# Tying the 32-column operations of the state-space parameters to VectorE's order in the first MLP's first part

## The chip, the cores and the metric

One core of one Trainium2 chip runs the whole program. The metric is the device time of one execution in microseconds (us): the median of several runs.

## The reference, cut to what matters

A causal decoder trunk of two layers on a sequence of 512 tokens of width 1024, all in float32. Each layer is a mixer and a gated MLP, both with a residual add behind an RMS norm. Layer 0 mixes by a convolution and attention, layer 1 by a state-space model (S5) whose parameters are worked out from 32 groups of 64 complex states.

```python
def conv_ffn(xn, w_up, conv_w, conv_b, w_down):          # width 2816, conv over 3 tokens
    h = causal_dwconv(xn @ w_up, conv_w, conv_b)
    return (jax.nn.silu(h[..., :D_FF]) * h[..., D_FF:]) @ w_down

def s5_mixer(xn, w_in, log_dt, a_re, a_im, b_re, b_im, c_re, c_im, d_skip, w_glu, b_glu):
    u = (xn @ w_in).astype(f32).reshape(bsz, s, SSM_GROUPS, SSM_GROUP)
    dt = jnp.exp(log_dt.astype(f32))[:, None]
    mag = jnp.exp(ar * dt)
    lb_re, lb_im = mag * jnp.cos(ai * dt), mag * jnp.sin(ai * dt)
    den = ar * ar + ai * ai
    f_re = (nr * ar + ni * ai) / den        # nr, ni = lb_re - 1, lb_im; f_im likewise
    bb_re = f_re[..., None] * br - f_im[..., None] * bi
    ...                                     # scan over the sequence, output map, GLU

for i in range(2):
    x = x + mixer(rms_norm(x, mix_g), *mix_params)
    x = x + conv_ffn(rms_norm(x, ffn_g), *ffn_params)
return rms_norm(x, final_norm)
```

What `s5_mixer` does ahead of the scan (dt, mag, the cosines, lb, f, bb and powers of lb) depends on no token. It is needed only in layer 1.

## The kernel before, in words

**Layout and matmuls.** Activations lie transposed: channels on the 128 partitions, the 512 tokens along the free axis, so x is eight tiles of 128x512. Every product is made of three float32r matmuls (`mm3`: high weight by high input, high by low, low by high), called from `mm` (L109).

**Weights.** `chunk` hands out 128x1024 pieces of the weights in the fixed list `order`, two ahead of use (`LOOK`). For each, `load_w` issues one transfer on SyncE's queue into `raw` (L114, two buffers), ScalarE casts it into `whi` (L124, three buffers) and GpSimd makes the rest `wlo` in four subtractions of 128x256 (L126, three buffers).

**Order of the work.** Each engine runs its own list in order. The Tile framework's scheduler makes these lists from a simulated timeline; the code's order decides only what the data need and how ties fall. Instructions that are passed to `held` (`keep_in_program_order`) keep the code's order among themselves on their engine. In the kernel before no VectorE operation of the part in question is held.

**Ahead of the MLP.** The attention mixer ends with the out projection: TensorE makes eight `wo`, VectorE adds each to x (L657). Behind each add the norm goes on, in the class `Norm`: ScalarE makes the high part `xh` and the square `sq`, VectorE the low part `xl` (L273) and the running sum `ssq` (L291, L293, L298). Then `wide()` closes it: `total` splits the sum (`th` on ScalarE, `tl` on VectorE, L233) and adds it over the partitions on TensorE (`sum`, L235), VectorE makes `m` (L303) and three Newton steps (L226 to L228) of nine operations of 128x512, which give `rb`, the norm's factor. TensorE needs `xh` and `xl` for the MLP, but not `rb`.

**The MLP.** `ffn(l, ...)` runs in three `PARTS` of 8, 8 and 6 column pairs. For each pair there are two branches: an up projection into `ua` or `ug` (24 matmuls), then on VectorE `h` = PSUM times `rb` (L931), on ScalarE the first tap of the convolution back into PSUM (L932), and on VectorE two more taps (L934, 128x511 and 128x510). ScalarE makes `sl` = silu (L943), VectorE `g` = `sl` times `ug` (L946), ScalarE the cast `ghl` (L949), GpSimd its low half (L950). Behind the pairs of a part come eight down projections `dn`, which need the `ghl` of all pairs of the part, and VectorE adds them to x (L958). In layer 0's first two parts one step of the list `extra` is run behind each `dn`.

**The parameters.** `s5_tables` gives that list. It first calls `s5_small` (L762 to L815): some 180 VectorE operations of mostly 128x32 (exponentials, sines, reciprocals, complex powers and squarings) that depend on each other in chains, plus 128x64 and 128x128 ones. The eight batches of `s5_batch` follow (`bc` loaded on SyncE's queue, L863; `bb`, `bt`, `wn`, `w2` on VectorE; `en` and `e2` on GpSimd, L887 to L889; `park_O` written back, L896). In the kernel before `s5_small` is called at the head of `ffn`, outside any loop, and the scheduler places its operations where it likes.

Of the kernel before, what the change touches and what calls it, by code (L numbers as in the profile page):

```python
# [71 lines left out]
def trunk(ctx, tc, A, out):  # L72
# [617 lines left out]
        t = tpool.tile([128, n, NG], F32, tag=name, name=name)  # L690
        return t if n > 1 else t[:, 0]

    tt, ts, stt = v.tensor_tensor, v.tensor_scalar, v.scalar_tensor_tensor

    def exp_small(dst, a):
        MAGIC = 12582912.0
        xc, k, r, q = sm("xc"), sm("k"), sm("r"), sm("q")
        sc = sm("sc", I32)
        ts(xc, a, -87.0, 88.0, ALU.max, ALU.min)
        ts(k, xc, 1.4426950408889634, MAGIC, ALU.mult, ALU.add)  # L700
        ts(k, k, -MAGIC, None, ALU.add)
        stt(r, k, -0.693359375, xc, ALU.mult, ALU.add)
        stt(r, k, 2.12194440054690583e-4, r, ALU.mult, ALU.add)
        ts(q, r, 1.0 / 5040, None, ALU.mult)
        for c in (1.0 / 720, 1.0 / 120, 1.0 / 24, 1.0 / 6, 0.5, 1.0):
            stt(q, q, c, r, ALU.add, ALU.mult)
        ts(sc, k, 127.0, 8388608.0, ALU.add, ALU.mult)
        stt(dst, q, 1.0, sc.bitcast(F32), ALU.add, ALU.mult)

    def unit(c, sn):  # L710
        m, t = sm("m"), sm("t")
        tt(m, c, c, ALU.mult)
        tt(t, sn, sn, ALU.mult)
        tt(m, m, t, ALU.add)
        ts(m, m, -0.5, 1.5, ALU.mult, ALU.add)
        tt(c, c, m, ALU.mult)
        tt(sn, sn, m, ALU.mult)

    def sincos_small(c, sn, th):
        MAGIC = 12582912.0  # L720
        k, r, f, q, u = sm("k"), sm("r"), sm("f"), sm("q"), sm("u")
        ts(k, th, 0.15915494309189535, MAGIC, ALU.mult, ALU.add)
        ts(k, k, -MAGIC, None, ALU.add)
        stt(r, k, -6.28125, th, ALU.mult, ALU.add)
        stt(r, k, -0.0019340515136718750, r, ALU.mult, ALU.add)
        stt(r, k, -1.2556659146019e-06, r, ALU.mult, ALU.add)
        ts(r, r, 0.125, None, ALU.mult)
        tt(f, r, r, ALU.mult)
        ts(q, f, -1.0 / 5040, None, ALU.mult)
        stt(q, q, 1.0 / 120, f, ALU.add, ALU.mult)  # L730
        stt(q, q, -1.0 / 6, f, ALU.add, ALU.mult)
        stt(sn, q, 1.0, r, ALU.add, ALU.mult)
        ts(q, f, -1.0 / 40320, None, ALU.mult)
        stt(q, q, 1.0 / 720, f, ALU.add, ALU.mult)
        stt(q, q, -1.0 / 24, f, ALU.add, ALU.mult)
        stt(u, q, 0.5, f, ALU.add, ALU.mult)
        for _ in range(3):
            t = sm("t")
            stt(t, u, -1.0, sn, ALU.add, ALU.mult)
            stt(u, sn, 2.0, sn, ALU.mult, ALU.mult)  # L740
            ts(sn, t, -2.0, None, ALU.mult)
        ts(c, u, -1.0, 1.0, ALU.mult, ALU.add)
        unit(c, sn)

    def cmul(dr, di, ar, ai, br, bi, mk):
        t1, t2 = mk("cm1"), mk("cm2")
        tt(t1, ar, br, ALU.mult)
        tt(t2, ai, bi, ALU.mult)
        tt(dr, t1, t2, ALU.subtract)
        t3, t4 = mk("cm3"), mk("cm4")  # L750
        tt(t3, ar, bi, ALU.mult)
        tt(t4, ai, br, ALU.mult)
        tt(di, t3, t4, ALU.add)

    rho = keep("rho")
    fre, sfi = keep("fre"), keep("sfi")
# [4 lines left out]

    def s5_small():  # L762
        dt, e = sm("dt"), sm("e")
        exp_small(dt, ldt)
        tt(e, are, dt, ALU.mult)
        mag = keep("mag")
        exp_small(mag, e)
        th = sm("th")
        tt(th, aim, dt, ALU.mult)
        c, sn = keep("c"), keep("sn")  # L770
        sincos_small(c, sn, th)
        v.memset(pr[:, 0], 1.0)
        v.memset(pi[:, 0], 0.0)
        tt(pr[:, 1], mag, c, ALU.mult)
        tt(pi[:, 1], mag, sn, ALU.mult)
        nr, d1, d2 = sm("nr"), sm("d1"), sm("d2")
        ts(nr, pr[:, 1], -1.0, None, ALU.add)
        tt(d1, are, are, ALU.mult)
        tt(d2, aim, aim, ALU.mult)
        tt(d1, d1, d2, ALU.add)  # L780
# [3 lines left out]
        tt(a1, nr, are, ALU.mult)
        tt(a2, pi[:, 1], aim, ALU.mult)
        tt(a1, a1, a2, ALU.add)
        tt(fre, a1, rd, ALU.mult)
        a3, a4 = sm("a3"), sm("a4")
        tt(a3, pi[:, 1], are, ALU.mult)
        tt(a4, nr, aim, ALU.mult)  # L790
        tt(a3, a3, a4, ALU.subtract)
        stt(sfi, a3, s1, rd, ALU.mult, ALU.mult)
        for lo, n in ((1, 1), (2, 2), (4, 4)):
            def mk(name):
                return tpool.tile([128, 4, NG], F32, tag="cm", bufs=2, name=name)[:, :n]
            bc = [128, n, NG]
            cmul(pr[:, lo + 1:lo + 1 + n], pi[:, lo + 1:lo + 1 + n], pr[:, 1:1 + n], pi[:, 1:1 + n],
                 pr[:, lo:lo + 1].to_broadcast(bc), pi[:, lo:lo + 1].to_broadcast(bc), mk)
        ts(spr, pr, s1, None, ALU.mult)
        for j in range(CL):  # L800
            v.tensor_copy(prr[:, j], pr[:, CL - 1 - j])
            ts(spir[:, j], pi[:, CL - 1 - j], s1, None, ALU.mult)
        r2 = sm("r2")
        tt(r2, mag, mag, ALU.mult)
        tt(r2, r2, r2, ALU.mult)
        tt(rho, r2, r2, ALU.mult)
        g.memset(tab["D"][:, :, 0:1], 0.0)
        g.tensor_copy(tab["D"][:, :, 1:], rho.unsqueeze(2).to_broadcast([128, NG, NC - 1]))
        for n in range(8):
            dst = (sm("wa"), sm("wb")) if n < 2 else (wr[:, n - 2], wi[:, n - 2])  # L810
            t1, t2 = sm("t1"), sm("t2")
            tt(t1, c, c, ALU.mult)
            tt(t2, sn, sn, ALU.mult)
            tt(dst[0], t1, t2, ALU.subtract)
            stt(dst[1], c, 2.0, sn, ALU.mult, ALU.mult)  # L815
            unit(*dst)
# [490 lines left out]
```

## Time and the profile before

| what | us |
|---|---|
| median of three runs | 1070.20 |
| the three runs | 1069.37, 1070.20, 1074.71 |
| the profiled execution's own time | 1072.81 |
| its span | 1071.0 |
| TensorE busy | 1025.4 (96%) |
| VectorE busy | 660.5 (62%) |
| GpSimd busy | 680.1 (63%) |
| ScalarE busy | 447.5 (42%) |

The profiled execution's time is 1.8 us over its span, and 2.6 us over the median. Positions in the text are microseconds from the span's start. In a row of a timeline the first number is that position, the second how long the instruction took, and a bracket behind it is the engine's idle time just before and what ended it. In the profile's names PE is TensorE, PEld its weight loads, DVE VectorE, ACT ScalarE, POOL GpSimd, SP SyncE.

### The profile page before, as it was taken

To read this page: it belongs to the slowest core of one execution; us is meant where nothing else is said; L and a number is where in the kernel's file an instruction comes from. 1 tells how busy PE (TensorE), PEld (TensorE's weight loads), DVE (VectorE), ACT (ScalarE), POOL (GpSimd) and SP (SyncE) were. 2 spreads that over 40 slices of the span, in tenths; PEclk is the share of its full clock that TensorE was granted. 3 is DMA by queue.
4 is the path that set the end of the run, shared out by engine and by line. 5 is a ranking of instruction groups with operands and counts; after the bars stand their busy time and mean duration, and the time that the engine had idled before them with its cause. 6 is when DMAs were issued, how large, how long until landed. Compare 5 with 4: busy or idle time off the path is not lost.

```text
span 1071.0 us, 14173 instructions
## 1 busy us (share of the span) xinstructions
PE 1025.4 (96%) x4966; PEld 826.2 (77%) x4966; DVE 660.5 (62%) x1271; ACT 447.5 (42%) x665; POOL 680.1 (63%) x827
## 2 busy tenths in 40 slices
PE   7998999988999999999999778999999999999996
PEld 5876567766888888878888656888888888888895
DVE  7679974999647996368745485776521444214435
ACT  5476964413542335323444223535431444214431
POOL 4898955556776876678655552867755666556650
PEclk9999999999999999999999889999999999999998
DMA  5322202322333423233323641322223222232222
GB/s 194 112 96 79 60 21 68 112 74 79 105 111 105 134 86 129 83 120 122 114 84 116 229 135 50 119 98 99 99 85 112 99 99 99 79 111 94 96 75 79
DMA packets 54599, 108.66 MB, mean 101 GB/s; under 512 B 20609, under 2 KB 28417, under 8 KB 54529
## 3 DMA queue, kind: packets, MB, share of 16 engines
q1 hardware_dynamic: 54528, 107.77, 30.4%
q8 instruction: 39, 0.64, 0.2%
q14 instruction: 32, 0.25, 0.1%
HBM read 98.31 MB, written 8.39 MB: 100 GB/s over the span
## 4 chain that ended last, share of the span: by engine, by line
PE 75%; DVE 15%; ACT 3%; DMA 2%; issue 2%; POOL 2%; SPq 0%; DVEq 0%; POOLq 0%; ACTq 0%
PE ug L109 20%; PE dn L109 20%; PE ua L109 20%; PE gl L109 4%; PE win L109 3%; POOL wlo L126 2%; DVE acc L410 2%; PE pv L590 1%; PE wo L109 1%; PE sc L560 1%; PE w L109 1%; PE pt L574 1%; PE kb L907 1%; DMA raw<-w 1%; ACT whi L124 1%
## 5 line engine op out<-in xcount | busy, mean ns | idle before, releaser
L126 POOL TENSOR_TENSOR wlo<-raw,whi 128x256 fp32r<-128x256 f32 x639 | 485.4, 792 | 246.8 <-ACT whi L124 226.9
L124 ACT CAST whi<-raw 128x1024 fp32r<-128x1024 f32 (+1 forms) x162 | 167.0, 1035 | 291.4 <-PE dn L109 87.7
L109 PE MATMUL dn<-ghl,whi 128*128 128x512 f32 (+1 forms) x632 | 192.9, 387 | 0.0
L109 PE MATMUL ug<-xh,whi 128*128 128x512 f32 x352 | 138.0, 392 | 5.7 <-ACT whi L124 4.2
L109 PE MATMUL ua<-xl,whi 128*128 128x512 f32 x352 | 137.4, 390 | 1.9 <-DVE xl L273 1.9
L109 PE MATMUL ug<-xh,wlo 128*128 128x512 f32 x352 | 137.9, 392 | 0.2
L109 PE MATMUL ua<-xh,whi 128*128 128x512 f32 x352 | 137.6, 391 | 0.0
L109 PE MATMUL ug<-xl,whi 128*128 128x512 f32 x352 | 137.5, 391 | 0.0
L109 PE MATMUL ua<-xh,wlo 128*128 128x512 f32 x352 | 137.1, 390 | 0.0
L109 PEld LDWEIGHTS dn<-ghl,whi 128*128 128x128 f32 x632 | 117.3, 188 | 24.6 <-issue 0.8
L109 PE MATMUL dn<-ghl,wlo 128*128 128x512 f32 (+1 forms) x316 | 121.8, 386 | 0.0
L958 DVE TENSOR_TENSOR x<-x,dn 128x512 f32<-128x512 f32 x40 | 26.8, 683 | 108.8 <-PE dn L109 108.8
L934 DVE SCALAR_TENSOR_TENSOR ug<-h,vec,ug 128x511 f32<-128x511 f32 x88 | 66.2, 753 | 42.7 <-ACT ug L932 41.4
L934 DVE SCALAR_TENSOR_TENSOR ua<-h,vec,ua 128x511 f32<-128x511 f32 x88 | 66.3, 753 | 41.3 <-ACT ua L932 39.9
L109 PEld LDWEIGHTS ug<-xh,whi 128*128 128x128 f32 x352 | 66.4, 189 | 20.9 <-ACT whi L124 5.1
L950 POOL TENSOR_TENSOR ghl<-g,ghl 128x512 fp32r<-128x512 f32 x44 | 57.1, 1297 | 34.3 <-ACT ghl L949 34.3
L109 PEld LDWEIGHTS ua<-xl,whi 128*128 128x128 f32 x352 | 66.3, 188 | 16.0 <-DVE xl L273 2.4
L109 PEld LDWEIGHTS ug<-xh,wlo 128*128 128x128 f32 x352 | 66.2, 188 | 14.7 <-POOL wlo L126 1.1
L109 PEld LDWEIGHTS ua<-xh,whi 128*128 128x128 f32 x352 | 66.1, 188 | 14.2 <-issue 0.6
L109 PEld LDWEIGHTS ug<-xl,whi 128*128 128x128 f32 x352 | 66.3, 188 | 13.7
L109 PEld LDWEIGHTS ua<-xh,wlo 128*128 128x128 f32 x352 | 66.2, 188 | 13.8
L109 PEld LDWEIGHTS dn<-ghl,wlo 128*128 128x128 f32 x316 | 59.4, 188 | 11.7
(343 smaller groups left out, 1788.0 us busy)
## 6 DMA issues: line engine op xcount, KB each, us to landing
raw<-up SPq DMA_DIRECT2D x88, 512.0 KB, 3.2
raw<-down SPq DMA_DIRECT2D x32, 512.0 KB, 3.3
raw<-w SPq DMA_DIRECT2D x14, 512.0 KB, 3.7
raw<-down SPq DMA_DIRECT2D x16, 384.0 KB, 2.9
raw<-wg SPq DMA_DIRECT2D x8, 512.0 KB, 3.5
raw<-wo_a SPq DMA_DIRECT2D x4, 512.0 KB, 3.2
raw<-wo_c SPq DMA_DIRECT2D x4, 512.0 KB, 4.2
park_O<-wn SPq DMA_DIRECT2D x8, 256.0 KB, 2.6
```

The source lines that it names most:

```text
L109: r = pe.matmul(*a, **kw)
L124: s.copy(hi[:, :n], r)
L126: (eng or g).tensor_tensor(lo[:, a:a + 2], r[:, a:a + 2], hi[:, a:a + 2].bitcast(F32), ALU.subtract)
L410: held(v.scalar_tensor_tensor(acc[:, sh:], u[:, :T - sh], col("cw", i * CK + CK - 1 - sh), acc[:, sh:], ALU.mult, ALU.add))
L560: pe.matmul(ps[:, :L], q[:, sl], k[:, :L], start=True, stop=False)
L574: pe.transpose(pt[:, kt * 128:(kt + 1) * 128], p[:, kt * 128:(kt + 1) * 128], ident)
L590: pe.matmul(ps[a, kt * 128:], vv[:, kt, i * 128 + 64 * e:i * 128 + 64 * e + 64], pts[e][:, 4 * kt:3 * kt + 4].rearrange("p k c -> p (k c)" ...
L907: pe.matmul(kb[0:16, i * 128:(i + 1) * 128], bb[:, i], wn[:, i, 0:8].rearrange("p j c -> p (j c)"), start=True, stop=True)
L934: v.scalar_tensor_tensor(ps[:, sh:], t[:, :T - sh], col(fw, 3 * j + 2 - sh), ps[:, sh:], ALU.mult, ALU.add)
L950: g.tensor_tensor(lo, gt, h.bitcast(F32), ALU.subtract)
L958: v.tensor_tensor(x[m], x[m], ps, ALU.add)
```

## The change

The functions of the small operations (`exp_small`, `unit`, `sincos_small`, `cmul`, `s5_small`) become generators that stop behind each operation. `pin` wraps `tensor_tensor`, `tensor_scalar` and `scalar_tensor_tensor`, so that the operation is `held` while `pinned[0]` is set, which it is from the head of `s5_small` to its end. `ffn` no longer calls them at once: `drip(14)` takes 14 steps ahead of each branch in every part, which lasts for the 16 branches of the first part, since there are 185 steps; `drip(1000)` ahead of the down projections takes what is left. No instruction is added or removed on any engine. All VectorE operations of the new code that go through `pin` are shown as L698.

```diff
+DRIP = 14
...
-    tt, ts, stt = v.tensor_tensor, v.tensor_scalar, v.scalar_tensor_tensor
+    pinned = [False]
+
+    def pin(op):
+        def run(*a):
+            r = op(*a)
+            return held(r) if pinned[0] else r
+        return run
+
+    tt, ts, stt = pin(v.tensor_tensor), pin(v.tensor_scalar), pin(v.scalar_tensor_tensor)
...
-        tt(m, c, c, ALU.mult)
-        tt(t, sn, sn, ALU.mult)
+        yield tt(m, c, c, ALU.mult)
+        yield tt(t, sn, sn, ALU.mult)
...
     def s5_tables(bp):
-        s5_small()
+        pinned[0] = True
+        yield from s5_small()
+        pinned[0] = False
...
-        return todo
+        yield todo
...
     def ffn(l, nrm, nxt, extra=None):
         rb = nrm.wide()
         fw, fb = f"fw{l}", f"fb{l}"
-        extra = [] if extra is None else extra(fp)
+        steps, extra = extra and extra(fp), []
+
+        def drip(n):
+            for _ in range(n):
+                r = next(steps, 0) if steps else 0
+                if r == 0:
+                    return
+                if isinstance(r, list):
+                    extra.extend(r)
...
             for i in range(i0, i0 + n):
+                drip(DRIP)
                 pa = branch(2 * i, bank("ua"))
                 sl = tmp("sl")
                 s.activation(sl, pa, AF.Silu)
+                drip(DRIP)
                 pg = branch(2 * i + 1, bank("ug"))
...
+            drip(1000)
             for m in range(KD):
```

What that does to the engines' lists is seen at three places. On VectorE, at the end of the out projection, the small operations stood between the adds and the norm's operations (numbers behind `x_`, `d_` and `cm_` are tile numbers):

```order
L657 TENSOR_TENSOR x_84<-x_84,wo 128x512
L715 TENSOR_SCALAR m<-m 128x32
L716 TENSOR_TENSOR c<-c,m 128x32
L717 TENSOR_TENSOR sn<-sn,m 128x32
L774 TENSOR_TENSOR pr<-mag,c 128x32
L775 TENSOR_TENSOR pi<-mag,sn 128x32
L777 TENSOR_SCALAR nr<-pr 128x32
L273 SCALAR_TENSOR_TENSOR xl<-x_82,vec,xh 128x512
L778 TENSOR_TENSOR d_2152<-ssm_small 128x32
```

Now that stretch of the list holds the adds and the norm alone up to the first branch:

```order
L299 TENSOR_TENSOR ssq<-ssq,sq 128x512
L234 TENSOR_TENSOR tl<-ssq,th 128x512
L304 TENSOR_SCALAR m<-sum 128x512
L225 TENSOR_SCALAR rb<-m 128x512
L227 TENSOR_TENSOR q<-rb 128x512
L228 SCALAR_TENSOR_TENSOR q<-q,m 128x512
L229 SCALAR_TENSOR_TENSOR rb<-q,rb 128x512
...
L698 TENSOR_SCALAR xc<-ssm_small 128x32
L952 TENSOR_TENSOR h<-ua,rb 128x512
```

Of the small operations only the first (`xc`) and one `wn` stay ahead of the first `h`; 206 of the 208 that stood there have gone. They stand between the branches' operations, up to the 16th branch. On VectorE at the tenth branch, where before only `h`, two taps and `g` stood, the list reads:

```order
L952 TENSOR_TENSOR h<-ug,rb 128x512
L698 TENSOR_TENSOR pi<-cm_2388,cm_2389 128x32
L698 TENSOR_TENSOR m<-m,t 128x32
L698 TENSOR_TENSOR cm_2393<-pr 128x64
L698 TENSOR_TENSOR cm_2394<-pi 128x64
L698 TENSOR_SCALAR spir<-pi,vec 128x32
L698 TENSOR_SCALAR m<-m 128x32
L698 TENSOR_TENSOR pr<-cm_2393,cm_2394 128x64
...
L955 SCALAR_TENSOR_TENSOR ug<-h,vec,ug 128x511
```

About 14 small operations stand in each branch, more in branches 8 to 11. On SyncE's queue the second `bc` and the first `park_O` stood among the loads of the up projection's weights:

```order
L114 DMA raw<-up 128x1024 x5
L863 DMA bc<-ssm_bc 128x256
L114 DMA raw<-up 128x1024
L896 DMA park_O<-wn 128x4x128
L114 DMA raw<-up 128x1024 x10
L114 DMA raw<-down_0 128x1024 x7
```

Now they follow all of these loads of the first part:

```order
L115 DMA raw<-up 128x1024 x16
L876 DMA bc<-ssm_bc 128x256
L909 DMA park_O<-wn 128x4x128
L115 DMA raw<-down_0 128x1024 x7
```

GpSimd's copy of `tabD`, `en` and `e2` move from ahead of the first low half of `ghl` to between the fourth and the sixth. From the first `dn` on, all five lists are as before.

## Rows read from the trace of the kernel before

**Rows 1.** The page's first section: busy time of each engine, its share of the span, instructions.

```profile
PE 1025.4 (96%) x4966; PEld 826.2 (77%) x4966; DVE 660.5 (62%) x1271; ACT 447.5 (42%) x665; POOL 680.1 (63%) x827
```

**Rows 2.** Busy time of each engine from the first `ua` to the first `dn` of the first MLP, and of the second MLP (layer 1, without parameter operations).

```profile
core 0: us, PE busy (x) PEld busy (x) DVE busy (x) ACT busy (x) POOL busy (x), PEclk, DMA share, GB/s
203.66:303.47 99.81, 91.30 (x388) 73.14 (x387) 87.81 (x229) 39.20 (x53) 62.65 (x75) 0.98 0.26 88
696.39:783.89 87.50, 87.50 (x388) 72.46 (x387) 55.01 (x72) 41.38 (x55) 58.62 (x72) 1.00 0.29 98
```

**Rows 3.** TensorE's timeline in the first of these stretches: three matmuls that waited.

```profile
209.83 0.50 PE L109 MATMUL ua<-xl,whi 128*128 128x512 f32 x1 [1.93 <-DVE xl L273]
239.09 0.50 PE L109 MATMUL ug<-xh,whi 128*128 128x512 f32 x1 [2.76 <-ACT whi L124]
252.05 0.50 PE L109 MATMUL ug<-xh,whi 128*128 128x512 f32 x1 [1.43 <-ACT sl L943]
```

**Rows 4.** SyncE's queue and ScalarE's timeline: when the second `bc` was issued, and the weight cast that waited behind it.

```profile
234.12 0.33 SPq L863 DMA_DIRECT2D bc<-ssm_bc  x1
237.99 1.05 ACT L124 CAST whi<-raw 128x1024 fp32r<-128x1024 f32 x1 [18.35 <-DMA raw<-up]
```

**Rows 5.** VectorE's timeline: the first and the last instruction of the stretch in which it had no idle time, and the busy times of all engines between them.

```profile
180.65 0.18 DVE L699 TENSOR_SCALAR xc<-ssm_small 128x32 f32<-128x32 f32 x1 [1.54 <-DMA ssm_small<-ssm]
266.78 0.68 DVE L931 TENSOR_TENSOR h<-ua,rb 128x512 f32<-128x512 f32 x1
180.65:266.78 86.13, 77.62 (x328) 61.79 (x327) 84.89 (x258) 27.52 (x36) 46.78 (x56) 0.98 0.30 96
```

**Rows 6.** VectorE's timeline among the last Newton operations: two small operations and a wide one (L228), which show the step from one start to the next.

```profile
242.97 1.27 DVE L812 TENSOR_TENSOR t<-wr 128x32 f32<-128x32 f32 x1
...
247.39 0.68 DVE L228 SCALAR_TENSOR_TENSOR rb<-q,rb 128x512 f32<-128x512 f32 x1
247.99 0.18 DVE L712 TENSOR_TENSOR m<-wr 128x32 f32<-128x32 f32 x1
```

**Rows 7.** VectorE's costliest groups from 180 to 266 us: line, operation, tile, shape, count, busy us, mean ns of one, idle before.

```profile
L273 DVE SCALAR_TENSOR_TENSOR xl<-x,vec,xh 128x512 fp32r<-128x512 f32 x8 | 6.4, 801 | 0.0
L657 DVE TENSOR_TENSOR x<-x,wo 128x512 f32<-128x512 f32 x8 | 5.4, 677 | 0.0
L293 DVE TENSOR_TENSOR ssq<-ssq,sq 128x512 f32<-128x512 f32 x5 | 3.4, 683 | 0.0
L227 DVE SCALAR_TENSOR_TENSOR q<-q,m 128x512 f32<-128x512 f32 x3 | 2.6, 881 | 0.0
L226 DVE TENSOR_TENSOR q<-rb 128x512 f32<-128x512 f32 x3 | 2.6, 877 | 0.0
L934 DVE SCALAR_TENSOR_TENSOR ua<-h,vec,ua 128x511 f32<-128x511 f32 x2 | 1.5, 749 | 0.0
```

**Rows 8.** Three places of the second MLP (the twin): its last add to x, its first `h`, and what VectorE waited for in its first part (us in all, count, longest).

```profile
700.36 0.76 DVE L1143 TENSOR_TENSOR x<-x,gz 128x512 f32<-128x512 f32 x1
720.36 0.69 DVE L931 TENSOR_TENSOR h<-ua,rb 128x512 f32<-128x512 f32 x1
DVE ua L934 <- ACT ua L932: 7.7, 8, 1.7
DVE ug L934 <- ACT ug L932: 7.2, 7, 2.1
```

**Rows 9.** The same places in the first MLP, and the end of its first part: last add, first `h`, eighth `g`, its cast, its low half, and the first matmul that reads that.

```profile
211.71 0.67 DVE L657 TENSOR_TENSOR x<-x,wo 128x512 f32<-128x512 f32 x1
248.20 0.68 DVE L931 TENSOR_TENSOR h<-ua,rb 128x512 f32<-128x512 f32 x1
309.93 0.69 DVE L946 TENSOR_TENSOR g<-sl,ug 128x512 f32<-128x512 f32 x1
310.66 0.62 ACT L949 CAST ghl<-g 128x512 fp32r<-128x512 f32 x1 [2.33 <-DVE g L946]
311.35 1.28 POOL L950 TENSOR_TENSOR ghl<-g,ghl 128x512 fp32r<-128x512 f32 x1 [0.75 <-ACT ghl L949]
313.53 0.48 PE L109 MATMUL dn<-ghl,whi 128*128 128x512 f32 x1
```

**Rows 10.** Two short stretches, with GpSimd busy throughout and idle throughout, and one small operation of the first.

```profile
220.20:226.20 6.00, 5.35 (x24) 4.43 (x24) 6.00 (x10) 0.00 (x0) 6.00 (x8) 1.00 0.00 0
226.30:229.70 3.40, 3.40 (x17) 2.81 (x16) 3.40 (x28) 0.00 (x0) 0.00 (x0) 1.00 0.02 5
222.79 0.78 DVE L874 TENSOR_TENSOR bt<-bc,sfi 128x64 f32<-128x64 f32 x1
```

**Rows 11.** GpSimd's costliest group from 180.65 to 266.78 us, and two runs of weight subtractions from its timeline, the second in the twin.

```profile
L126 POOL TENSOR_TENSOR wlo<-raw,whi 128x256 fp32r<-128x256 f32 x51 | 38.7, 788 | 31.8 <-ACT whi L124 31.8
254.67 2.83 POOL L126 TENSOR_TENSOR wlo<-raw,whi 128x256 fp32r<-128x256 f32 x4 [1.12 <-ACT whi L124]
707.58 12.20 POOL L126 TENSOR_TENSOR wlo<-raw,whi 128x256 fp32r<-128x256 f32 x12 [5.17 <-ACT whi L124]
```

**Rows 12.** The granted clock (the column behind the engines) around the first wait of rows 3.

```profile
209.00:214.00 5.00, 4.17 (x11) 3.29 (x12) 5.00 (x17) 3.43 (x6) 2.73 (x3) 0.66 0.07 27
```

More of the change, by code (lines that the diff above doesn't have):

```diff
@@ L698, in exp_small @@
         sc = sm("sc", I32)
[L699 to L704, printed above, removed]
+        yield ts(xc, a, -87.0, 88.0, ALU.max, ALU.min)
+        yield ts(k, xc, 1.4426950408889634, MAGIC, ALU.mult, ALU.add)
+        yield ts(k, k, -MAGIC, None, ALU.add)
+        yield stt(r, k, -0.693359375, xc, ALU.mult, ALU.add)
+        yield stt(r, k, 2.12194440054690583e-4, r, ALU.mult, ALU.add)
+        yield ts(q, r, 1.0 / 5040, None, ALU.mult)
         for c in (1.0 / 720, 1.0 / 120, 1.0 / 24, 1.0 / 6, 0.5, 1.0):
-            stt(q, q, c, r, ALU.add, ALU.mult)
-        ts(sc, k, 127.0, 8388608.0, ALU.add, ALU.mult)
-        stt(dst, q, 1.0, sc.bitcast(F32), ALU.add, ALU.mult)
+            yield stt(q, q, c, r, ALU.add, ALU.mult)
+        yield ts(sc, k, 127.0, 8388608.0, ALU.add, ALU.mult)
+        yield stt(dst, q, 1.0, sc.bitcast(F32), ALU.add, ALU.mult)
     def unit(c, sn):
         m, t = sm("m"), sm("t")
-        tt(m, c, c, ALU.mult)
-        tt(t, sn, sn, ALU.mult)
[L714 to L717, printed above, removed]
+        yield tt(m, c, c, ALU.mult)
+        yield tt(t, sn, sn, ALU.mult)
+        yield tt(m, m, t, ALU.add)
+        yield ts(m, m, -0.5, 1.5, ALU.mult, ALU.add)
+        yield tt(c, c, m, ALU.mult)
+        yield tt(sn, sn, m, ALU.mult)
     def sincos_small(c, sn, th):
@@ L721, in sincos_small @@
         k, r, f, q, u = sm("k"), sm("r"), sm("f"), sm("q"), sm("u")
[L722 to L736, printed above, removed]
+        yield ts(k, th, 0.15915494309189535, MAGIC, ALU.mult, ALU.add)
+        yield ts(k, k, -MAGIC, None, ALU.add)
+        yield stt(r, k, -6.28125, th, ALU.mult, ALU.add)
+        yield stt(r, k, -0.0019340515136718750, r, ALU.mult, ALU.add)
@@ new lines, in sincos_small @@
+        yield stt(r, k, -1.2556659146019e-06, r, ALU.mult, ALU.add)
+        yield ts(r, r, 0.125, None, ALU.mult)
+        yield tt(f, r, r, ALU.mult)
+        yield ts(q, f, -1.0 / 5040, None, ALU.mult)
+        yield stt(q, q, 1.0 / 120, f, ALU.add, ALU.mult)
+        yield stt(q, q, -1.0 / 6, f, ALU.add, ALU.mult)
+        yield stt(sn, q, 1.0, r, ALU.add, ALU.mult)
+        yield ts(q, f, -1.0 / 40320, None, ALU.mult)
+        yield stt(q, q, 1.0 / 720, f, ALU.add, ALU.mult)
+        yield stt(q, q, -1.0 / 24, f, ALU.add, ALU.mult)
@@ L737, in sincos_small @@
+        yield stt(u, q, 0.5, f, ALU.add, ALU.mult)
         for _ in range(3):
             t = sm("t")
[L739 to L743, printed above, removed]
+            yield stt(t, u, -1.0, sn, ALU.add, ALU.mult)
+            yield stt(u, sn, 2.0, sn, ALU.mult, ALU.mult)
+            yield ts(sn, t, -2.0, None, ALU.mult)
+        yield ts(c, u, -1.0, 1.0, ALU.mult, ALU.add)
@@ L745, in cmul @@
+        yield from unit(c, sn)
     def cmul(dr, di, ar, ai, br, bi, mk):
         t1, t2 = mk("cm1"), mk("cm2")
-        tt(t1, ar, br, ALU.mult)
-        tt(t2, ai, bi, ALU.mult)
-        tt(dr, t1, t2, ALU.subtract)
+        yield tt(t1, ar, br, ALU.mult)
+        yield tt(t2, ai, bi, ALU.mult)
+        yield tt(dr, t1, t2, ALU.subtract)
         t3, t4 = mk("cm3"), mk("cm4")
-        tt(t3, ar, bi, ALU.mult)
-        tt(t4, ai, br, ALU.mult)
-        tt(di, t3, t4, ALU.add)
+        yield tt(t3, ar, bi, ALU.mult)
@@ L755, in trunk @@
+        yield tt(t4, ai, br, ALU.mult)
+        yield tt(di, t3, t4, ALU.add)
     rho = keep("rho")
@@ L763, in s5_small @@
         dt, e = sm("dt"), sm("e")
-        exp_small(dt, ldt)
-        tt(e, are, dt, ALU.mult)
+        yield from exp_small(dt, ldt)
+        yield tt(e, are, dt, ALU.mult)
         mag = keep("mag")
-        exp_small(mag, e)
+        yield from exp_small(mag, e)
         th = sm("th")
-        tt(th, aim, dt, ALU.mult)
+        yield tt(th, aim, dt, ALU.mult)
         c, sn = keep("c"), keep("sn")
-        sincos_small(c, sn, th)
+        yield from sincos_small(c, sn, th)
         v.memset(pr[:, 0], 1.0)
         v.memset(pi[:, 0], 0.0)
-        tt(pr[:, 1], mag, c, ALU.mult)
-        tt(pi[:, 1], mag, sn, ALU.mult)
+        yield tt(pr[:, 1], mag, c, ALU.mult)
+        yield tt(pi[:, 1], mag, sn, ALU.mult)
         nr, d1, d2 = sm("nr"), sm("d1"), sm("d2")
[L777 to L780, printed above, removed]
+        yield ts(nr, pr[:, 1], -1.0, None, ALU.add)
+        yield tt(d1, are, are, ALU.mult)
+        yield tt(d2, aim, aim, ALU.mult)
+        yield tt(d1, d1, d2, ALU.add)
         rd = sm("rd")
@@ L783, in s5_small @@
         a1, a2 = sm("a1"), sm("a2")
[L784 to L787, printed above, removed]
+        yield tt(a1, nr, are, ALU.mult)
+        yield tt(a2, pi[:, 1], aim, ALU.mult)
+        yield tt(a1, a1, a2, ALU.add)
+        yield tt(fre, a1, rd, ALU.mult)
         a3, a4 = sm("a3"), sm("a4")
[L789 to L792, printed above, removed]
+        yield tt(a3, pi[:, 1], are, ALU.mult)
+        yield tt(a4, nr, aim, ALU.mult)
+        yield tt(a3, a3, a4, ALU.subtract)
+        yield stt(sfi, a3, s1, rd, ALU.mult, ALU.mult)
         for lo, n in ((1, 1), (2, 2), (4, 4)):
@@ L811, in s5_small @@
             t1, t2 = sm("t1"), sm("t2")
[L812 to L816, printed above, removed]
+            yield tt(t1, c, c, ALU.mult)
+            yield tt(t2, sn, sn, ALU.mult)
+            yield tt(dst[0], t1, t2, ALU.subtract)
+            yield stt(dst[1], c, 2.0, sn, ALU.mult, ALU.mult)
+            yield from unit(*dst)
             c, sn = dst
     def s5_tables(bp):
-        s5_small()
+        pinned[0] = True
+        yield from s5_small()
+        pinned[0] = False
         kz = bp.tile([16, 128], F32, name="kz")[:, :112]
```

18 lines of the change are left out of this document (10 added, 8 removed).

## The prediction, made before the changed kernel was run

> **What bounds the kernel now.** The page's busy times come first: TensorE is busy for 96% of the span [rows 1], so a change that touches VectorE alone can gain only where TensorE waits. The busy times by stage show one such place next to the change. From the first `ua` to the first `dn` the first MLP takes 99.81 us, its twin in layer 1 with the same 388 matmuls 87.50 us; the difference is that VectorE has 229 instructions in the one and 72 in the other [rows 2]. So 12.3 us is all that the change can give back in this stage.
>
> TensorE's timeline says whom it waits for there: `xl` of VectorE, `whi` of ScalarE, `sl` of ScalarE [rows 3]. The longest of them, 2.76 us for `whi` at 239.09, hangs on VectorE too: SyncE's queue issued the second `bc` only at 234.12 and held the up loads behind it, and the cast then waited 18.35 us in all for its `raw` [rows 4]. (`bc` waits for a buffer that `wn` and `bt` on VectorE read.)
>
> VectorE's timeline closes the argument. From 180.65 to the `h` at 266.78 it has no idle time [rows 5]; the small operations, the norm and the first branches share 86.1 us. It is saturated there. The question is thus not whether the small operations leave the norm's chain, which the lists show, but whether VectorE can finish the same work by the time at which the first `dn` needs it.
>
> **The change part by part.** No instruction is added, and TensorE's work from the first `dn` on is as before. I sum VectorE's work up to the eighth `g`, which the last low half of `ghl` needs.
>
> *Price of a small operation.* The stretch of 86.1 us holds 49 wide operations: 8 adds, 8 `xl`, 7 of `ssq`, `tl`, `m`, the first `rb`, 9 Newton, 4 `h`, 8 taps, 2 `g`. Their durations [rows 7], some 0.7 us for those without a row, sum to 35.7 us. A wide one of 0.68 us lets the next start 0.60 us after it [rows 6], so 0.08 goes off each: 31.7 us. The other 54.4 us belong to some 208 small ones, 0.262 us each.
>
> *The norm's chain gets shorter.* In the twin, where nothing stands in it, the first `h` comes 20.0 us behind the last add (700.36 to 720.36) [rows 8]. Before, it took 36.5 us here (211.71 to 248.20) [rows 9]. TensorE's out projection ends at 203.66, so the last add falls at about 204.0, and the first `h` at 224.0: 24.2 us earlier.
>
> *The work then is behind it.* From there on VectorE owes 16 `h` at 0.60, 32 taps at 0.67 and 8 `g` at 0.60, 35.8 us, and 206 small operations at 0.262, 54.0 us. With no idle time the eighth `g` ends at 224.0 + 35.8 + 54.0 = 313.8. Before, it was done at 310.6 (309.93 and 0.69) [rows 9]. That is 3.2 us later, although the chain ends 24.2 us earlier: from 180.65 to 224 VectorE used to fill its waits for `wo` and for the sum with small operations, and now it stands idle there.
>
> *What sets the price.* A small operation takes about 0.12 us where GpSimd is idle (28 instructions in 3.40 us), and 0.7 to 0.8 where GpSimd is busy, as `bt` with 0.78 [rows 10], or the `t` of 1.27 us between Newton operations [rows 6]. With x free and y caught ones, 0.12x + 0.70y = 54.4 and x + y = 208 give y = 51, for 46.78 us of GpSimd's work in the stretch [rows 5], 1.08 for each us. In the new place GpSimd's list holds 48 subtractions of `wlo` and 7 of `ghl` beside the small operations, where it had 51 and 1: 6 x 1.28 [rows 9] less 3 x 0.79 [rows 11] is 5.3 us more. That is 5.7 more caught at 0.58, so 3.3 us. The eighth `g` ends at 317.1.
>
> *From there to TensorE.* The cast and the low half behind that `g` end 2.0 us later (312.63), and TensorE read the pair at 313.53 [rows 9]. In the new kernel that is 319.1 at the earliest, 5.6 us later, and everything behind it is TensorE's, in the same order. So +5.6 us.
>
> *Edits taken at nothing.* The held order costs nothing by itself as far as a chain goes, since each runs in the code's order anyway. VectorE's waits for ScalarE's first tap, 7.7 and 7.2 us in the twin [rows 8], are filled by small operations; if none were, 14.9 us is what it costs, and that is the upper bound. `en`, `e2` and the `tabD` copy move on GpSimd to between the fourth and sixth low half, covered by its idle time in the stretch (86.1 less 46.8 us) [rows 5]; if that cover is gone, at most the time of their neighbour, 1.28 us a piece, falls on a `ghl` that is needed only at the end. On SyncE's queue `bc` and `park_O` now follow all sixteen up loads, so the loads are no longer held (the 2.76 us go), but a `down` load may stand behind `park_O`, which waits for VectorE's `wn`; that is done before the eighth `g`. TensorE's clock: around the first wait [rows 3] the granted clock was 0.66 for 5 us [rows 12], the lower of the two levels for part of it; at that price a wait costs up to 1.7 us more. TensorE by itself would read the last pair 10 us (303.47 to 313.53) behind 203.66 + 87.5, at 301.2; the 17.9 us up to 319.1 are spread over sixteen branches, 1.1 us each, and the clock of the whole stage with five waits of 0.7 to 2.8 us was 0.98 [rows 2], so I take nothing.
>
> **Sum.** 3.2 + 3.3 - 0.9 (the slack between 312.63 and 313.53) = +5.6 us. Against the profiled execution, 1072.81, that gives 1078.4. This execution stands 2.6 us above the median of the three runs, so I put the forecast at 1070.2 + 5.6 = 1075.8.
>
> **Rivals.**
>
> *The small operations get cheaper in the new place (faster).* They then fall into VectorE's waits for ScalarE and into GpSimd's pauses. With a mean price p TensorE reads the last pair at 261.8 + 206p. My forecast is p = 0.278. The other side begins at p = 0.251 (313.5); it is faster by 5.4 us from p = 0.225; and at p = 0.191 TensorE never waits for VectorE, which gives the whole 12.3 us, 1057.9. For it: 0.12 is the price with GpSimd idle [rows 10]. Against it: GpSimd has more to do there, not less.
>
> *GpSimd is slowed as well (slower still).* In the twin twelve subtractions took 12.20 us, 1.02 each; beside small operations four took 2.83, 0.71 each [rows 11]. If in the new place each takes 1.02, some 50 us of GpSimd's work become 72, catch 24 more operations at 0.58, and add 13.8 us: 1089.6. Against it: the 12.20 us were beside wide VectorE operations, and the 2.83 beside small ones. The Trainium skill has the rule for this, in "SBUF — State Buffer", section "Who interferes with whom": a VectorE instruction with two SBUF inputs and a GpSimd one that reads SBUF compete for one pair of ports, and whoever issues first keeps it for the whole instruction. By that rule the 0.7 us of a caught operation is GpSimd's instruction running out, with which the mean of 0.788 us agrees [rows 11], and GpSimd can be blocked likewise.
>
> *It is absorbed (no change).* TensorE runs ahead through the branches, meets the late `ghl` with other `dn` matmuls to do, and ends where it did: 1070.2. For it: the first `dn` started 10 us ahead of the matmul that read the last pair (303.47 and 313.53) [rows 2, 9]. Against it: that slack was used up before as well.
>
> **How the numbers follow.** Forecast 0.60, cheaper operations 0.20, slowed GpSimd 0.10, absorbed 0.10. A measurement of this kernel tells no less than 0.5% from no change, 5.4 us: faster is below 1064.8, slower above 1075.6. The forecast lies just on that bound, so 0.35 of its 0.60 goes to slower and 0.25 to no change. Of the cheaper case 0.12 is faster and 0.08 within the bound. Together: faster 0.12, within 0.43, slower 0.45. The range begins at p = 0.23, 4.3 us earlier than before, 1066, and ends where half of the 14.9 us of waits for ScalarE come on top, 1075.8 + 7.5, 1084 with the clock's part.
>
> **What the profile would show.** Right: the first `h` at about 224, VectorE without idle time from there to the eighth `g` at 314 to 320, small operations of 0.12 and of 0.7 us mixed, TensorE waiting in most branches for VectorE, and the matmul that reads the last pair at about 319. Wrong in size: a mean price under 0.25 in the new place. Wrong in kind: VectorE with idle time in the middle branches, the eighth `g` before 305, or a wait in TensorE behind a `down` load.

## The result and the profile after

The changed kernel takes 1082.53 us (median of 1080.02 to 1085.65) beside 1070.45 for the kernel before: ratio 1.0109, 95% interval 1.0079 to 1.0139, so 12.1 us slower, by the interval 8.5 to 14.9. The forecast was +5.6. The profiled execution took 1085.65, 3.1 over its median; its span is 1083.9, 12.9 more than before. First the same places as in [rows 5, 8, 9] on VectorE: last add, a Newton operation, first `h`, a small operation of the second pair, eighth `g`.

```profile
207.42 0.67 DVE L658 TENSOR_TENSOR x<-x,wo 128x512 f32<-128x512 f32 x1
...
224.81 1.11 DVE L229 SCALAR_TENSOR_TENSOR rb<-q,rb 128x512 f32<-128x512 f32 x1
225.84 0.71 DVE L698 TENSOR_SCALAR xc<-ssm_small 128x32 f32<-128x32 f32 x1
226.47 0.68 DVE L952 TENSOR_TENSOR h<-ua,rb 128x512 f32<-128x512 f32 x1
...
235.66 1.17 DVE L698 SCALAR_TENSOR_TENSOR r<-k,xc 128x32 f32<-128x32 f32 x1
...
321.19 0.69 DVE L969 TENSOR_TENSOR g<-sl,ug 128x512 f32<-128x512 f32 x1
```

The norm's chain has become short: the first `h` stands at 226.47, not 248.20 [rows 9]. The eighth `g` is nevertheless 11.3 us later (321.88 against 310.62). GpSimd in the same stretch, with the subtractions beside Newton operations (222.25) and beside branches (236.74), and the low half behind that `g`:

```profile
222.25 4.26 POOL L127 TENSOR_TENSOR wlo<-raw,whi 128x256 fp32r<-128x256 f32 x4 [1.03 <-ACT whi L125]
...
235.46 1.33 POOL L973 TENSOR_TENSOR ghl<-g,ghl 128x512 fp32r<-128x512 f32 x1 [1.36 <-ACT ghl L972]
236.74 2.83 POOL L127 TENSOR_TENSOR wlo<-raw,whi 128x256 fp32r<-128x256 f32 x4
...
322.60 1.28 POOL L973 TENSOR_TENSOR ghl<-g,ghl 128x512 fp32r<-128x512 f32 x1 [3.45 <-ACT ghl L972]
```

In the branches a subtraction takes 0.71 us, as in [rows 11] at 254.67: GpSimd is not slowed by the tied operations. The small `r` of 1.17 us is, it ran beside the `ghl` at 235.46.

TensorE's timeline, all its waits from 204 to 326, and the matmul that answers to 313.53 in [rows 9]:

```profile
277.92 0.79 PE L110 MATMUL ug<-xh,whi 128*128 128x512 f32 x1 [7.32 <-ACT whi L125]
...
308.84 0.50 PE L110 MATMUL dn<-ghl,whi 128*128 128x512 f32 x1 [2.62 <-ACT ghl L972]
310.19 0.79 PE L110 MATMUL dn<-ghl,whi 128*128 128x512 f32 x1 [0.85 <-DVE m L698]
...
322.58 0.79 PE L110 MATMUL dn<-ghl,whi 128*128 128x512 f32 x1 [5.53 <-ACT ghl L972]
...
324.52 0.78 PE L110 MATMUL dn<-ghl,whi 128*128 128x512 f32 x1
```

Where five waits of 0.7 to 2.8 us stood, three of them in [rows 3], there are now four, and two are long. The first of them is VectorE's work too, seen in ScalarE's timeline ahead of it:

```profile
274.84 0.60 ACT L965 ACTIVATE sl<-ua 128x512 f32<-128x512 f32 x1 [6.20 <-DVE ua L955]
276.12 0.78 ACT L953 ACTIVATE ug<-h,vec 128x512 f32<-128x512 f32 x1 [0.68 <-DVE h L952]
276.84 1.03 ACT L125 CAST whi<-raw 128x1024 fp32r<-128x1024 f32 x1
```

ScalarE runs its list in order: the cast of the next weights stands behind a `sl` that waited 6.20 us for VectorE's taps. Busy times and granted clock by window (the number behind the five engines):

```profile
180.65:203.66 23.01, 23.01 (x103) 19.05 (x102) 11.35 (x16) 11.69 (x16) 15.09 (x20) 1.00 0.52 142
203.66:226.00 22.34, 22.34 (x101) 18.48 (x99) 19.20 (x22) 7.82 (x10) 18.09 (x19) 1.00 0.33 113
...
275.00:280.00 5.00, 2.08 (x5) 1.69 (x6) 5.00 (x25) 2.19 (x3) 2.06 (x3) 0.50 0.32 105
280.00:285.00 5.00, 5.00 (x17) 3.96 (x17) 5.00 (x19) 2.36 (x3) 2.07 (x3) 0.71 0.33 105
...
320.00:325.00 5.00, 2.42 (x7) 2.02 (x8) 1.84 (x5) 0.62 (x1) 1.28 (x1) 0.54 0.29 105
325.00:330.00 5.00, 5.00 (x19) 3.92 (x18) 1.38 (x2) 2.48 (x3) 3.55 (x6) 0.78 0.00 0
```

The third engine is VectorE. From 180.65 to 226 it is idle for 14.8 us, where it had no idle time before [rows 5]; that is the time which the change throws away. Behind each long wait the granted clock is below 1 for a while: 0.50 in the window from 275, the lower of its two levels (1.2 and 2.4 GHz), and 0.71 in the next, the lower one for part of it.

A sum over 5 us windows tells what TensorE loses in a kernel: its idle time, plus its busy time times one less the granted clock (my estimate of the clock's part). From 180 to 440 us:

| kernel | idle | clock | time against before |
|---|---|---|---|
| before | 8.5 | 1.7 | |
| changed | 16.3 | 6.5 | 1.0109 |
| e1, changed without small operations | 0.7 | 0.0 | 0.9900 |
| e6, before without small operations (e1's lists) | 0.7 | 0.0 | 0.9897 |
| e7, before with memsets | 2.4 | 1.6 | 0.9924 |
| e2, changed with memsets | 5.0 | 2.1 | 0.9951 |
| e12, two places, fewer | 8.1 | 0.0 | 1.0011 |
| e11, two places | 9.1 | 3.4 | 1.0043 |
| e5, in the down projections | 12.0 | 6.0 | 1.0082 |
| e10, before, GpSimd's queue | 15.0 | 2.2 | 1.0091 |
| e8, DRIP = 28 (the changed kernel's lists) | 16.0 | 7.2 | 1.0098 |
| e4, tied early | 12.1 | 5.1 | 1.0111 |
| e9, e5 on GpSimd's queue | 13.8 | 5.7 | 1.0112 |
| e3, DRIP = 7 | 16.8 | 6.4 | 1.0122 |

Before loses 10.2, the changed kernel 22.8: the difference, 12.6, is nearly the whole 12.9 of the spans.

### The profile page after: what moved, and what is told of

The parts are those of the page before. It is cut to its first block, busy times and chain, and to the rows that moved or that the text cites. A ratio compares the mean times of both kernels' runs of the same rounds, so it can differ in the third digit from the quotient of the medians.

```text
span 1083.9 us, 14176 instructions
## 1 busy us (share of the span) xinstructions
PE 1032.0 (95%) x4966; PEld 831.1 (77%) x4966; DVE 667.9 (62%) x1271; ACT 448.6 (41%) x665; POOL 685.1 (63%) x827
## 4 chain that ended last, share of the span: by engine, by line
PE 75%; DVE 16%; ACT 2%; DMA 2%; issue 2%; POOL 2%; SPq 0%; DVEq 0%; ACTq 0%; POOLq 0%
PE dn L110 19%; PE ua L110 19%; PE ug L110 18%; PE wo L110 4%; PE gl L110 4%; PE win L110 3%; DVE acc L411 2%; POOL wlo L127 1%; PE pv L591 1%; PE sc L561 1%; DVE ug L955 1%; DVE ua L955 1%; PE w L110 1%; DVE h L952 1%; PE q L110 1%
## 5 line engine op out<-in xcount | busy, mean ns | idle before, releaser
L127 POOL TENSOR_TENSOR wlo<-raw,whi 128x256 fp32r<-128x256 f32 x639 | 490.4, 799 | 245.7 <-ACT whi L125 225.1
L110 PE MATMUL dn<-ghl,whi 128*128 128x512 f32 (+1 forms) x632 | 196.1, 392 | 9.0 <-ACT ghl L972 8.2
L973 POOL TENSOR_TENSOR ghl<-g,ghl 128x512 fp32r<-128x512 f32 x44 | 57.2, 1300 | 46.5 <-ACT ghl L972 46.4
L972 ACT CAST ghl<-g 128x512 fp32r<-128x512 f32 x44 | 27.3, 621 | 103.8 <-DVE g L969 103.8
```

What stands on the lines that cost most here:

```text
L110: r = pe.matmul(*a, **kw)
L127: (eng or g).tensor_tensor(lo[:, a:a + 2], r[:, a:a + 2], hi[:, a:a + 2].bitcast(F32), ALU.subtract)
```

## The experiments

The theory: a small operation has its price wherever it runs; what counts is how much of VectorE's time is left before the eighth `g`. The change moves small operations from time in which VectorE waited anyway (180 to 226) to time in which others wait for VectorE. The rivals: the moved transfers and the lists of SyncE and ScalarE; the tie itself; a price that has nothing to do with GpSimd. The change without its tie was not run: its lists on all five engines are the kernel before's, so the tie is what moves everything. By the changed lists the first tied operation stands right behind the norm's last, which is also where the code emits it.

The first rival is met by the trace of the changed kernel itself. In the kernel before, ScalarE's casts waited for held up loads (the first row; us in all, count, longest, from 204 to 326 in each kernel). In the changed one no cast waits for a transfer in that time; its longest waits are for VectorE:

```profile
ACT whi L124 <- DMA raw<-up: 20.3, 2, 18.4
```

```profile
ACT ghl L972 <- DVE g L969: 26.1, 8, 5.5
ACT sl L965 <- DVE ua L955: 15.6, 4, 6.2
```

And from the first `h` to the end of the eighth `g` VectorE, the third engine, is busy for 93.76 of 95.41 us, so that its waits for other engines and transfers held that `g` up by no more than 1.65 us (what GpSimd adds to an operation lies in the busy time):

```profile
226.47:321.88 95.41, 79.76 (x330) 64.07 (x328) 93.76 (x263) 33.68 (x44) 52.46 (x64) 0.92 0.25 82
```

**e1 and e6: the small operations left out, in both kernels.**

```diff
     def s5_small():
-        dt, e = sm("dt"), sm("e")
-        ...
+        for t in (fre, sfi, pr, pi, spr, prr, spir, wr, wi, rho):
+            v.memset(t, 0.5)
+        g.memset(tab["D"], 0.5)
```

> The changed kernel with the small operations of s5_small left out: their results are set to a constant by ten memsets, everything behind them (batches, tables) stays. Theory T (VectorE is short of time: deferred small operations take it from the 16 branches, and TensorE ends up waiting for the eighth g): VectorE then owes 35.8 us behind the first h at about 225 and has idle time; the matmul on the last pair is read at about 302 instead of 324.5, so 1082.5 - 22.5 = 1060, below the kernel before (1070.5) by about 10. Rival S (the loss comes from the moved transfers on SyncE's queue and ScalarE's order, which this kernel keeps): no less than 1075.

> The kernel before with the small operations left out, as in e1 (results set to a constant). Theory T: both kernels differ only in where the small operations lie, so this one is at e1's 1060 (1058 to 1062): the small operations cost 10 to 12 us in the kernel before and 22 in the changed one. Rival S (the moved transfers and the tie have an effect of their own): it differs from e1 by over 4 us.

Measured 1060.31 and 1060.35 (0.9900, interval 0.9883 to 0.9917, and 0.9897, 0.9879 to 0.9915). Without small operations the two programs are the same, instruction for instruction on all five engines, and in both the second `bc` and the first `park_O` go out between 184 and 190, ahead of the up loads. Its expectation says that e1 keeps the moved transfers; it does not, and that the two times agree tells nothing about that rival. What the pair does give is the price of the small operations with all that hangs on their place: 10.7 to 11.0 us in the kernel before and 22 in the changed one. TensorE's waits from 180 to 440 in e1:

```profile
PE ua L110 <- DVE xl L274: 0.4, 1, 0.4
```

**e2 and e7: GpSimd reads nothing for the first part's weights, in both kernels.**

```diff
-            (eng or g).tensor_tensor(lo[:, a:a + 2], r[:, a:a + 2], hi[...], ALU.subtract)
+            if plain:    # the 16 up chunks of the first part
+                g.memset(lo[:, a:a + 2].bitcast(F32), 0.0)
+            else:
+                ...                  # the subtraction, as it was
```

> The changed kernel with GpSimd's 64 subtractions for the low weight halves of the first part's up projections replaced by memsets to 0 (GpSimd then reads nothing there; the low halves of the products are left out). All 185 tied operations stay. Theory T with contention as the price: a small operation costs about 0.13 us instead of 0.29, so 206 x 0.16 = 33 us less VectorE time, the eighth g is done by about 289 to 295, TensorE does not wait for it: about 1060 (to 1064). Rival C (the price of a small operation in the new place is VectorE's own, by dependence between neighbours and fixed cost): 1080 to 1083, mean price still 0.25 or more.

> The kernel before with the memsets of e2 in place of the 64 weight subtractions of the first part. Theory T: the contention price falls here too; VectorE's backlog ahead of the first h shrinks by about 35 x 0.55 = 20 us, the first h comes at about 230, and TensorE's 12.3 us of waits go: 1059 to 1063, and less than e2. Rival (contention hits only the new place): 1068 or more.

Measured 1066.27 (0.9951, 0.9932 to 0.9969) and 1062.91 (0.9924, 0.9910 to 0.9937). No VectorE operation was touched, and the changed kernel became 16 us faster. Its first `h` comes at 220.3 instead of 226.5, and 203 small operations take 45.9 us instead of 57.3. (In e2 the scheduler orders some matmuls and a few VectorE operations otherwise; in e7 the lists of TensorE, VectorE and ScalarE are the kernel before's, and the first `h` comes at 233.15 instead of 248.20.) GpSimd and VectorE in e2, one small operation beside a `ghl`, one beside memsets:

```profile
229.31 1.32 POOL L978 TENSOR_TENSOR ghl<-g,ghl 128x512 fp32r<-128x512 f32 x1 [3.35 <-ACT ghl L977]
...
235.74 1.07 POOL L128 MEMSET wlo<- 128x256 f32 x4 [4.10 <-PE ug L110]
```

```profile
229.52 1.17 DVE L703 SCALAR_TENSOR_TENSOR r<-k,xc 128x32 f32<-128x32 f32 x1
...
236.03 0.18 DVE L703 SCALAR_TENSOR_TENSOR r<-k,th 128x32 f32<-128x32 f32 x1
```

The counts say the same: of 47 small operations that ran beside weight subtractions alone in the changed kernel 30 took over 0.45 us, of 33 beside memsets alone in e2 one did, and of 126 with no GpSimd instruction beside them none did, in either. So GpSimd's reading sets the price. The Trainium skill says so, in "SBUF — State Buffer", section "Who interferes with whom": a VectorE instruction with two SBUF inputs contends with a GpSimd instruction that reads SBUF, not with one that only writes it; the two rows agree. The expected 0.13 us for each operation was too low, it was 0.226: a free one takes 0.14 from its start to the next, but 21 are still caught, most of them by `ghl`, `en` and later weights, and e2 stayed above the 1060 to 1064 expected.

**e3: half as many at each branch** (`DRIP = 7`).

> DRIP = 7 instead of 14: by the lists 79 small operations then stand behind the eighth g, among the first four adds of the down projections, the rest is as in the changed kernel. Theory T: the eighth g comes 79 x 0.29 = 23 us earlier, at about 300, and TensorE reads the last pair at about 302 without waiting; the 79 operations then take 23 us in the down projections, where VectorE was 80% idle, and hold the first adds by about 10 us; the gain is 12 to 22 us against the changed kernel: 1060 to 1070. Rival D (the operations cost the same wherever they lie up to the first batches, because the first adds or the first transposes of en wait for them): 1078 to 1083.

Measured 1084.49 (1.0122, 1.0105 to 1.0138): the theory's number was wrong, in two ways. First, the eighth `g` ends at 311.5, 10.4 us earlier, not 23: the 130 small operations left took 43.9 us, 0.338 each and not 0.29, since GpSimd caught 35 of them, beside 45 of 203 in the changed kernel (steps over 0.45 us counted from one start to the next), and VectorE was idle for 5.4 us among them. Second, VectorE had less room in the down projections than expected (in the changed kernel it is busy there for 7.0 of the 16 us from 324 to 340, not for a fifth), and 37 of the rest stand ahead of the first add of the down projections, which comes at 327.54; TensorE then waits for the tables:

```profile
338.47 1.09 PE L916 MATMUL ept<-ident,en 128*128 128x128 f32 x4 [4.27 <-DVE m L698]
```

**e8: twice as many at each branch** (`DRIP = 28`).

> DRIP = 28: the same tied operations in the first 7 branches. Theory T2: VectorE has no idle time up to the eighth g in the changed kernel, so the place within the 16 branches does not matter as long as it stays saturated; with fewer GpSimd instructions beside small operations some of them are not caught; the eighth g at 310 to 322: 1072 to 1083. Rival (even spreading is what matters, bunches stall TensorE's banks): 1087 or more.

Measured 1081.85 (1.0098, 1.0084 to 1.0111). The lists of all five engines are the changed kernel's, instruction for instruction: the scheduler puts the tied operations at the same places, whether the code hands it 14 or 28 at each branch. So e8 is the changed kernel once more (203 small operations in 57.2 us, the eighth `g` at 319.9). Its number came as expected, but nothing was moved, and whether the place within the saturated stretch matters stays open. Nor do about 14 stand in each branch in either program: there are 6 to 11 behind each of the first seven `h`, 14 to 26 behind the next four, and 10 to 18 behind the four that follow.

**e4: the same tied operations ahead of the norm.**

```diff
         taps(1000)
+        pinned[0] = True
+        for _ in s5_small():
+            pass
+        pinned[0] = False
```

> The same tied operations, but emitted at once behind the convolution's taps in the attention mixer (their tiles in a pool of their own, so that their inputs can be loaded at the start) instead of 14 at each branch. VectorE has some 20 us of idle time between 150 and 185 in the trace of before. Theory T: what counts is in which idle time of VectorE the operations lie, so 20 us of the backlog go; the first h comes at 230 to 240, and most of the 12.3 us that TensorE waited in the kernel before go: 1059 to 1065, faster than both kernels. Rival H (the tie itself costs: held operations keep others waiting on VectorE): no better than before, 1070 or more.

Measured 1083.89 (1.0111, 1.0089 to 1.0133): wrong. The first tied operation starts at 171.16 only, behind the last `xl` of the attention, and VectorE's idle time ahead of that stays empty. Then GpSimd is busy throughout. VectorE at 171, and the busy times around it:

```profile
171.16 1.29 DVE L372 TENSOR_SCALAR xc<-ssm_small 128x32 f32<-128x32 f32 x1
172.49 1.22 DVE L372 TENSOR_SCALAR k<-xc 128x32 f32<-128x32 f32 x1
```

```profile
171.00:180.00 9.00, 9.00 (x42) 7.43 (x41) 8.66 (x12) 5.01 (x8) 8.65 (x10) 1.00 0.11 37
```

Eleven small operations in 9 us: idle time of VectorE is worth little while GpSimd works. The rest delays the adds (the last at 224.53, not 211.71 [rows 9]), and the first `h` comes at 257.4. Whether the tie as such costs is not told apart here: it is the adds' place in the list that does.

**e5 and e9: behind the adds of the down projections.**

```diff
-                drip(DRIP)              # at both branches
...
+                if part == 1 and extra:
+                    extra.pop(0)()
...
+                elif part == 0:
+                    drip(24 if m < KD - 1 else 1000)
```

> The same 185 tied operations, none at the branches of the first part: 24 steps behind each add of its eight down projections; the 16 table steps move to part 1, one behind each pair and one behind each down projection. Theory T2 (as T, with the correction from e3 that operations ahead of the adds hold the down projections): the branches run as in the kernel without small operations, the last pair is read at about 302; the adds of the down projections come up to 15 us late, which TensorE's free PSUM banks cover; 1060 to 1066, faster than both kernels. Rival D (they cost the same wherever VectorE's consumers wait): 1070 or more, with waits of dn for x adds of 10 us or more.

> e5 with the transfers of bc and park_O issued on GpSimd's queue instead of SyncE's, where bc held the up loads of part 1 from 316 to 345.77 in e5. Theory T2: e5 lost its gain to that hold (a wait of 6.7 us for whi at 351 and a granted clock of 0.80 for 35 us, 7 us) and to 7.7 us of waits for the tables (kb). Without the hold 1066 to 1071. Rival (part 1 is simply short of VectorE time): 1077 or more.

Measured 1081.76 (1.0082, 1.0067 to 1.0098) and 1084.30 (1.0112, 1.0086 to 1.0139). The first half of the theory holds: from 204 to 330 TensorE has no wait in either, so without small operations in the branches the changed kernel's waits up to there are gone. Then e5, whose table steps also move, loses 6.7 us in one wait behind SyncE's queue and 7.7 us in waits for the tables. The queue, with `bc` waiting for VectorE and the up loads behind it (the second row is ScalarE):

```profile
345.77 0.33 SPq L876 DMA_DIRECT2D bc<-ssm_bc  x1
```

```profile
350.31 1.04 ACT L125 CAST whi<-raw 128x1024 fp32r<-128x1024 f32 x1 [20.91 <-DMA raw<-up]
```

In e9 that hold is gone, and other waits stand in its place: 3.6 us for `whi`, 2.8 for `wlo`, 10.6 for the tables. Its expectation failed. The waits stand where the tables now lie, between the branches of part 1; whether VectorE is short of time there was not tried by itself.

**e10: the kernel before with `bc` and `park_O` on GpSimd's queue.**

```diff
-        nc.sync.dma_start(out=bc, in_=A["ssm_bc"][b])
+        nc.gpsimd.dma_start(out=bc, in_=A["ssm_bc"][b])      # park["O1"] likewise
```

> The kernel before with the transfers of bc and park_O issued on GpSimd's queue, nothing else edited. It tells what the hold on SyncE's queue (up loads behind bc until 234.12) is worth in the kernel before. Theory T2: it is a symptom of VectorE's backlog; the waits for whi of 2.76 and 1.47 us go, at most 4 us: 1066 to 1070. Rival (most of the 12.3 us of TensorE's waits come from that hold): 1058 to 1063. Rival (GpSimd's issuing costs time beside its subtractions): 1073 or more.

Measured 1082.90 (1.0091, 1.0066 to 1.0116), slower, against the theory's number. The loads are no longer held, TensorE runs ahead, and meets VectorE's backlog in one piece. ScalarE and TensorE:

```profile
249.42 0.78 ACT L932 ACTIVATE ua<-h,vec 128x512 f32<-128x512 f32 x1 [17.36 <-DVE h L931]
```

```profile
254.64 0.79 PE L109 MATMUL ug<-xh,whi 128*128 128x512 f32 x1 [7.19 <-DVE wi L717]
```

The profile names the last to end, `wi`; ScalarE's cast of these weights, behind that `ua` in its list, ended 0.05 us ahead of the matmul. The hold on the queue was a symptom: the first `h` is at 248.7 as before. Of the 10.9 us the idle time of TensorE up to 440 makes 6.5; why the eighth `g` also comes 2.7 us later was not settled. The rival of GpSimd's issuing gave the right side (1073 or more). In the first part the two issues take 0.60 and 0.77 us and GpSimd then idles for 11.44 us, so they don't make these waits; for the later ones it stays open.

**e11 and e12: both places.** Some operations tied behind each add of the out projection (`few(8)`, `few(6)`), the rest at the branches (`DRIP` 8, 6); e12 also leaves 42 operations out.

```diff
                 v.tensor_tensor(x[m], x[m], ps, ALU.add)
+                few(8)
...
-            yield from unit(*dst)
+            if n == 3:                  # e12 only
+                yield from unit(*dst)
```

> The tied operations in both places: 8 behind each of the eight adds of the out projection (tied there, so behind the add; their tiles in a pool of their own), the other 121 steps at DRIP = 8 at the 16 branches. Theory T2 (VectorE's time up to the eighth g decides, and about 45 small operations are caught by GpSimd in the branches whatever their number): VectorE's idle time from 180 to 204 is used, the first h comes at about 229, 120 operations with 45 caught take 120 x 0.16 + 45 x 0.55 = 44 us, the eighth g at 229 + 35.8 + 44 = 309, the last pair read at 311.5: 1066 to 1071. Rival (each operation keeps its 0.28 us, or ties cost by themselves): no better than half way, 1076 or more.

> As e11, with 6 operations behind each add of the out projection and DRIP = 6, and with 42 small operations fewer: of the eight squarings only the fourth is followed by the renormalisation (unit). Theory T2: some 115 small operations are left behind the first h at about 228, spread evenly; with 42 caught they cost 115 x 0.16 + 42 x 0.55 = 41.5 us, the eighth g comes at 305 and the last pair is read at 307.5, 6 us ahead of the kernel before; no single wait of TensorE is over 4 us, so its clock stays high: 1064 to 1069, faster than both kernels. Rival (a fixed 0.28 us for each operation, or the even tie costs ScalarE's order): the last pair at 313 or later, 1070 or more.

Measured 1076.77 beside 1071.99 (1.0043, 1.0026 to 1.0059) and 1073.33 beside 1072.87 (1.0011, 0.9998 to 1.0024). The direction is the theory's: with VectorE's time at 180 to 204 used, most of the loss goes. The size is not. The eighth `g` ends at 313.2 and 311.3 where 309 and 305 were expected: the first `h` comes some 2 us late, at 230.7 and 230.2, and VectorE has 6.65 and 6.06 us of idle time behind it, which the theory had set at none. That about 45 operations are caught whatever their number was wrong as well, the other way: 28 of 136 were in e11 and 26 of 113 in e12. In e12 TensorE's longest wait is 1.87 us and its clock stays at 1.00, as expected; that short waits keep it there is not shown, since in the kernel before one of 1.93 us [rows 3] goes with a stretch at 0.66 [rows 12]. No version was found that beats the kernel before with all its operations.

## Why the prediction was right, and where its size was off

**Right: the mechanism.** From the first `h` to the eighth `g` VectorE is idle for only 1.65 of 95.41 us, and it idles from 180 to 226 instead. With the small operations behind the pairs (e5) TensorE has no wait in the branches.

**Right in sum, in part by luck: the price.** 206 operations were put at 54.0 + 3.3 = 57.3 us; 203 small ones took 57.3. The split was off both ways: 45 caught ones, not 57, at 0.78 us and not 0.70, and 0.14 us for a free one, not 0.12.

**Off: the first `h`**, 226.47 instead of 224.0. The step "the last add falls at about 204.0" failed: in VectorE's list two `xl` and one `ssq` stand between the last two adds, 3.0 us (204.37 to 207.42) beside GpSimd's subtractions. From there the chain took 19.05 us, against the 20.0 of the twin [rows 8].

**Off: VectorE's debt behind it**, 95.4 us instead of 93.1. The wide operations took 38.1 with the last `g`, instead of 35.8, since three of the tables' operations of 128x512 are among them, which I had counted as small.

**Off: from the `g` to the pair**, 2.65 us instead of 2.0. The three together are 2.5 + 2.3 + 0.65 = 5.4, which with the forecast 5.6 gives the 11.0 between 313.53 and 324.52.

**Off: TensorE's clock, taken at nothing.** The step "the 17.9 us up to 319.1 are spread over sixteen branches, 1.1 us each" failed: in the branches TensorE waited once, 7.32 us, and then 2.62, 0.85 and 5.53 in the down projections. Up to the pair the clock's loss is hidden, because VectorE sets that time; behind it the window 325 to 330 at 0.78 costs 1.1 of the 1.9 us by which the end is later than the pair. The rest, 0.8, is not told apart from what differs between two executions of one kernel.

**The range held by luck.** 1082.53 lies near the upper end of 1066 to 1084. That end stood for half of the 14.9 us in which VectorE waits for ScalarE, and those waits did not come. What made up the time instead are the terms above and the clock.

**The rivals.** Cheaper operations: no, 0.28 us each. GpSimd slowed as well: not in the branches, 0.71 us for a subtraction as before; beside the Newton operations it is, 4.26 us for four. Absorbed: no, TensorE has no work left at 322.

## What to carry to other kernels

Cleaning a critical chain by moving fillers pays only if the new place has idle time before the next deadline: add up the engine's whole debt up to that deadline. Count idle time together with what a neighbour engine does in it. Look at which in-order lists turn a late result into one long wait: the changed kernel and e10 each have a wait of TensorE of over 7 us, where the longest in the kernel before is 2.76. And compare the lists before the times: e1 and e6 are one program, and so are e8 and the changed kernel, and neither pair tells apart what it was meant to.

## What the runs showed of the hardware that was not expected

With the same 63 or 64 GpSimd instructions beside them, about a fifth to a quarter of the small operations was caught, however many they were: 45 of 203 in the changed kernel, 35 of 130 (e3), 28 of 136 (e11), 26 of 113 (e12). Where GpSimd was busy throughout, one small operation took 0.84 us on the mean (10.1 us for 12, e4), seven times its price with GpSimd idle [rows 10].
